# A router kernel's last row: one load in place of two, and three tiles of another split

## The chip, the cores and the metric

The kernel runs on one core of a Trainium2 chip. The metric is the time of one execution on the device in microseconds (us), the median of three runs. A core has TensorE (PE in the profile, its weight loads PEld), VectorE (DVE), ScalarE (ACT), GpSimd (POOL) and SyncE (SP), each with its own queue of instructions, and DMA engines that move data between HBM and the on-chip memory SBUF. Matmuls write into PSUM, from which VectorE and ScalarE read.

## The reference

The kernel computes a softmax over 8 scores per token. There are 16 x 512 = 8192 tokens of 1024 values.

```python
def reference(x: np.ndarray, router_weights: np.ndarray) -> np.ndarray:
    logits = np.matmul(x, router_weights)
    exp_logits = np.exp(logits - np.max(logits, axis=-1, keepdims=True))
    return (exp_logits / np.sum(exp_logits, axis=-1, keepdims=True)).astype(np.float32)
```

x has shape 16 x 512 x 1024 in fp32, router_weights 1024 x 8 in fp32.

## The kernel before

The 8192 tokens are laid out as 128 partitions of J = 64 rows each: partition p holds tokens 64p to 64p + 63. "Block j" is row j of every partition, 128 tokens of 1024 values. A block has KO = 8 column tiles of 128 x 128.

**Loads.** The first four blocks come in fp32 over SP's queue, and ScalarE casts them to bf16. All others are issued by GpSimd, whose DMAs cast to bf16 on the way: twelve loads of four blocks, three of two, five of one (`LOADS`, line 38), and for the last block two loads of 6 and 2 column tiles (`LAST_LOADS`, line 39, issued at line 86). All loads have buffers of their own. From the ninth on, an issue waits for the landing of the load eight before it[...].

**Per block.** `turn` transposes the 8 column tiles on TensorE into a PSUM tile `pt` (line 162, pool `psum_t`, four buffers). `evict` copies it to SBUF as `xT` (line 173). Up to block 53 (`NEAR`) VectorE copies all 1024 columns; after that VectorE takes 640 and ScalarE 384. `project` (line 114) multiplies the eight 128 x 128 pieces with the weights, 8 columns each, accumulating in a logits tile `lg` (pool `psum_l`, three buffers). It lags one or two blocks behind (`pend`). `fill` adds matmuls on constant data in blocks 24 to 59.

**Softmax.** Blocks are grouped for it (`GROUPS`, line 40): six groups of 8, one of 6, one of 8 and the last two blocks alone. The five steps of a group (`peak`, `power`, `total`, `recip`, `scale`) go into the list `later`, from which `step` takes one per block. The last two blocks have a softmax of their own (lines 210 to 223): the peak of each on VectorE (line 214), the exponent on ScalarE (line 215), then sum, reciprocal and scaling on VectorE.

**Order.** The schedule is written out by hand (`manual_schedule`): each engine executes its instructions in the order of the program text. For the last two blocks J-2 and J-1 that order is: transposes and copies of J-2, transposes of J-1 (three `pt` tiles: 4 tiles for VectorE and 2 for ScalarE from the first load, 2 for VectorE from the second), projections of J-2, copies of J-1, projections of J-1.

**Stores.** SP waits for the first of the last two loads by a DMA of two values (`mark`, line 194), then stores blocks 0 to 53 (line 195). The other ten blocks are stored at the very end (line 224).

Of the kernel before, what the change touches and what calls it, by code (L numbers as in the profile page):

```python
# [10 lines left out]
def kernel(  # L11
# [6 lines left out]
    nc = tc.nc  # L18
    P = 128
# [4 lines left out]
    KO = D // P  # L24
    J = M // P


    x_rows = x.rearrange("b s d -> (b s) d").rearrange("(p j) d -> p j d", p=P)
# [3 lines left out]
    bf16 = mybir.dt.bfloat16  # L32
# [2 lines left out]
    ALU = mybir.AluOpType  # L35


    LOADS = [4] * 13 + [2, 2, 2] + [1] * 5
    LAST_LOADS = [6, 2]
    GROUPS = [8] * 6 + [6, 8, 1, 1]  # L40
    assert sum(LOADS) == J - 1 and sum(LAST_LOADS) == KO and sum(GROUPS) == J
    DONE = sum(GROUPS[:7])
    NEAR = 54

# [1 line left out]
    xpool = ctx.enter_context(tc.tile_pool(name="x", bufs=1))  # L46
    xtp = ctx.enter_context(tc.tile_pool(name="xT", bufs=5))
    sm = ctx.enter_context(tc.tile_pool(name="sm", bufs=2))
    psum_t = ctx.enter_context(tc.tile_pool(name="psum_t", bufs=4, space=bass.MemoryType.PSUM))
    psum_f = ctx.enter_context(tc.tile_pool(name="psum_f", bufs=1, space=bass.MemoryType.PSUM))  # L50
    psum_l = ctx.enter_context(tc.tile_pool(name="psum_l", bufs=3, space=bass.MemoryType.PSUM))

    x_of = []
    with tc.manual_schedule():
# [3 lines left out]
        w_bf = const.tile([P, KO, N], bf16)  # L58
# [3 lines left out]

        x_f32 = const.tile([P, LOADS[0], D], fp32)
        for k in range(0, LOADS[0], 2):
            nc.sync.dma_start(out=x_f32[:, k:k + 2, :], in_=x_rows[:, k:k + 2, :])
        nc.scalar.dma_start(
            out=w8[:], in_=router_weights.rearrange("(ko ki) n -> ko ki n", ko=KO)
        )
        j0 = 0
        for i, r in enumerate(LOADS):  # L70
            xb = xpool.tile([P, r, D], bf16, name=f"x_{i}", tag=f"x_{i}")
# [7 lines left out]
            if i == 2:  # L79
                make_identity(nc, ident)  # L80
                nc.gpsimd.memset(filler[:], 0.5)  # L81
        x_last = []
        k0 = 0
        for i, n in enumerate(LAST_LOADS):
            xb = xpool.tile([P, n * P], bf16, name=f"xe_{i}", tag=f"xe_{i}")
            nc.gpsimd.dma_start(out=xb[:], in_=x_rows[:, J - 1, k0 * P:(k0 + n) * P])  # L86
            x_last.append((xb, k0, n))
            k0 += n
        nc.vector.tensor_copy(out=identity[:], in_=ident[:])  # L89
        w_ps = psum_l.tile([P, 8, N], fp32, name="lg")  # L90
        for n in range(N):
# [5 lines left out]
        logits = {}  # L97
# [9 lines left out]
        def project(j, parts):  # L107

            g, k = group_of[j]
            if g not in logits:  # L110
                logits[g] = psum_l.tile([P, 8, N], fp32, name="lg")
            for xT, k0, n in parts:
                for i in range(n):
                    nc.tensor.matmul(  # L114
                        logits[g][:, k, :],
                        lhsT=xT[:, i, :],
                        rhs=w_bf[:, k0 + i, :],
                        start=(k0 + i == 0),
                        stop=(k0 + i == KO - 1),
                    )  # L120
            if k == GROUPS[g] - 1 and j < J - 2:
                softmax(g)

        def softmax(g):
            n, a = GROUPS[g], first[g]
            lg = logits.pop(g)[:, 0:n, :]
            mx = sm.tile([P, n, 1], fp32, name="mx")
            ex = sm.tile([P, n, N], fp32, name="ex")
            ev = sm.tile([P, n, N], fp32, name="ev")
            ssum = sm.tile([P, n, 1], fp32, name="ssum")  # L130
            inv = sm.tile([P, n, 1], fp32, name="inv")

            def peak():
                nc.vector.reduce_max(mx[:, :, 0], lg, axis=X)  # L134

            def power():
                nc.vector.tensor_tensor(  # L137
                    out=ex[:], in0=lg, in1=mx[:].broadcast_to([P, n, N]), op=ALU.subtract
                )
                nc.scalar.activation(ev[:], ex[:], func=Exp)  # L140

            def total():
                nc.vector.reduce_sum(ssum[:, :, 0], ev[:], axis=X)  # L143

            def recip():
                nc.vector.reciprocal(inv[:], ssum[:])  # L146

            def scale():
                nc.vector.tensor_tensor(  # L149
                    out=outv[:, a:a + n, :], in0=ev[:], in1=inv[:].broadcast_to([P, n, N]), op=ALU.mult  # L150
                )

            later.extend([peak, power, total, recip, scale])

        def turn(xb, split, k0=0):

            pts, i = [], 0
            for copy, n in zip((nc.vector.tensor_copy, nc.scalar.copy), split):
                if n:
                    pt = psum_t.tile([P, KO, P], bf16, name="pt")  # L160
                    for c in range(n):
                        nc.tensor.transpose(  # L162
                            pt[:, c, :], xb[:, (i + c) * P:(i + c + 1) * P], identity[:]
                        )
                    pts.append((copy, pt, k0 + i, n))
                    i += n
            return pts

        def evict(pts):
            parts = []  # L170
            for copy, pt, k0, n in pts:
                xT = xtp.tile([P, n, P], bf16, name=f"xT{n}")
                copy(out=xT[:], in_=pt[:, 0:n, :])  # L173
                parts.append((xT, k0, n))
            return parts

        def step(n=1):
            for _ in range(n):
                if later:
                    later.pop(0)()  # L180

        for j in range(J - 2):
            xb, k = x_of[j]
            parts = evict(turn(xb[:, k, :], (KO, 0) if j < NEAR else (5, 3)))
            step()
            pend.append((j, parts))
            while len(pend) > (2 if j < NEAR else 1):
                project(*pend.pop(0))
            if 24 <= j < J - 4:
                fill(2 if j < 48 else 1)  # L190


        mark = const.tile([1, 2], bf16)
        nc.sync.dma_start(out=mark[:], in_=x_last[0][0][0:1, 0:2])
        nc.sync.dma_start(out=out_rows[:, 0:DONE, :], in_=outv[:, 0:DONE, :])


        while pend:
            project(*pend.pop(0))
        step(2)  # L200
        xb, k = x_of[J - 2]
        before = evict(turn(xb[:, k, :], (5, 3)))
        step(1)
        (xa, ka, na), (xb, kb, nb) = x_last
        turned = turn(xa, (4, 2), ka) + turn(xb, (2, 0), kb)
        project(J - 2, before)
        last = evict(turned)
        step(1)
        project(J - 1, last)
        low = sm.tile([P, 2], fp32, name="low")  # L210
        ev = sm.tile([P, 2, N], fp32, name="ev_last")
        for k in range(2):
# [9 lines left out]
            out=outv[:, J - 2:J, :], in0=ev[:], in1=ssum[:].broadcast_to([P, 2, N]), op=ALU.mult  # L222
# [32 lines left out]
```

## Time and profile before

| | |
|---|---|
| median of three runs | 88.85 us (88.81 to 88.88) |
| span of the profiled execution | 87.0 us (time of that run 88.78 us) |
| PE, PEld busy | 73%, 62% |
| DVE, ACT, POOL busy | 55%, 14%, 15% |
| read from HBM | 33.59 MB, 389 GB/s over the span |
| GpSimd's load queue | 15.73 MB written, 88.3% of 16 DMA engines' time |

The span is the time from the first to the last event of the profiled execution on the core; the time of a run contains a little more. The chain of waits follows the work that ended last back to the start, so its shares say what the span is made of. A timeline row gives start, duration, engine, line and operation with the tile written and the tile read, and in brackets the idle time ahead of it and what ended it. A row with "x8" is eight instructions in one piece, and its duration runs from the first one's start to the last one's end.

### The profile page before, as it was taken

How to read it: one execution, taken by the hardware profiler on the slowest of the kernel's cores; microseconds unless marked ns; L12 is line 12 of the kernel's file. 1: busy time of each engine (PE TensorE's matmuls, PEld its weight loads, DVE VectorE, ACT ScalarE, POOL GpSimd, SP SyncE). 2: the span in 40 equal slices, each digit the busy share in tenths (PEclk: the TensorE clock that was granted, in tenths of full speed). 3: DMA queues.
4: the chain of work that ended last, by engine and by line, in shares of the span. 5: the costliest groups of instructions: out<-in, count | busy, mean ns of one | idle time of the engine just before them, and what ended most of it. 6: DMA issues, size and time to landing. Idle time of an engine off the chain costs nothing.

```text
span 87.0 us, 2427 instructions
## 1 busy us (share of the span) xinstructions
PE 63.8 (73%) x1092; PEld 53.6 (62%) x1092; DVE 48.1 (55%) x112; ACT 12.4 (14%) x25; POOL 12.9 (15%) x29
## 2 busy tenths in 40 slices
PE   0408004999396926949999998989898999997730
PEld 0407004999296926947777775757575888795620
DVE  0303300699576663723677677746676589563760
ACT  3235009000100010000010001000100003454540
POOL 5990002020010202020010202020010222000000
PEclk9999999999956999555999999999999999999997
DMA  3899999999999999999999999999999999999520
GB/s 60 328 358 286 260 249 222 222 211 230 196 222 211 222 215 211 226 207 215 218 215 226 200 226 215 207 226 207 226 207 198 220 213 210 202 210 211 88 102 19
DMA packets 3773, 18.26 MB, mean 210 GB/s; under 512 B 556, under 2 KB 940, under 8 KB 1972
## 3 DMA queue, kind: packets, MB, share of 16 engines
q0 software_dynamic: 3168, 15.73, 88.3%
q1 hardware_dynamic: 580, 2.36, 7.3%
q8 instruction: 8, 0.13, 0.5%
q10 hardware_dynamic: 16, 0.03, 0.2%
q14 instruction: 1, 0.01, 0.0%
HBM read 33.59 MB, written 0.26 MB: 389 GB/s over the span
## 4 chain that ended last, share of the span: by engine, by line
DMA 89%; POOL 3%; issue 2%; DVE 1%; PE 1%; ACT 0%; POOLq 0%
DMA x<-in_x_dram 75%; DMA xe<-in_x_dram 14%; POOL x L76 2%; POOL filler L81 1%; DVE xT L173 0%; PE lg L114 0%; PE pt L162 0%; POOL ident masks.py:199 0%; ACT ev_last L215 0%; POOL ident masks.py:197 0%; DVE ssum_last L219 0%; DVE low L214 0%; DVE ssum_last L220 0%; DVE outv L221 0%; POOLq L239 0%
## 5 line engine op out<-in xcount | busy, mean ns | idle before, releaser
L173 DVE COPY xT<-pt 128x1024 bf16<-128x1024 bf16 (+2 forms) x65 | 42.0, 652 | 31.8 <-PE pt L162 31.6
L162 PE MATMUL pt<-identity,x 128*128 128x128 bf16 x504 | 43.4, 236 | 16.0 <-ACT x L74 8.1
L162 PEld LDWEIGHTS <-x 128*128 128x128 bf16 x504 | 34.6, 105 | 25.8 <-DMA x<-in_x_dram 10.9
L114 PE MATMUL lg<-w_bf,xT 128*128 128x8 bf16 x512 | 22.7, 168 | 0.3 <-DVE xT L173 0.2
L114 PEld LDWEIGHTS <-xT 128*128 128x128 bf16 x512 | 20.7, 99 | 0.5 <-DVE xT L173 0.5
L104 PE MATMUL spare<-filler 128*128 128x512 bf16 x60 | 19.2, 384 | 0.0
L76 POOL DMA_DIRECT2D x<-in_x_dram x20 | 10.7, 543 | 56.2 <-DMA x<-in_x_dram 55.4
L140 ACT ACTIVATE ev<-ex 128x64 f32<-128x64 f32 (+1 forms) x8 | 2.0, 255 | 56.2 <-DVE ex L137 56.2
L173 ACT COPY xT<-pt 128x384 bf16<-128x384 bf16 (+1 forms) x10 | 4.7, 467 | 5.1 <-PE pt L162 4.9
L74 ACT CAST x<-x_f 128x1024 bf16<-128x1024 f32 x4 | 4.0, 1042 | 8.5 <-DMA x_f<-in_x_dram 8.5
L104 PEld LDWEIGHTS <-filler 128*128 128x128 bf16 x60 | 4.1, 96 | 0.0
L92 PE MATMUL lg<-ident,w 8*128 8x8 f32 x8 | 1.0, 254 | 3.1 <-POOL ident masks.py:199 3.1
L92 PEld LDWEIGHTS lg<-ident,w 8*128 8x128 f32 x8 | 1.0, 198 | 3.1 <-POOL ident masks.py:199 3.1
L89 DVE CAST identity<-ident 128x128 bf16<-128x128 f32 x1 | 0.5, 512 | 3.0 <-POOL ident masks.py:199 3.0
L134 DVE TENSOR_REDUCE mx<-lg 128x8 f32<-128x64 f32 (+1 forms) x8 | 1.7, 213 | 0.5 <-PE lg L114 0.5
L137 DVE TENSOR_TENSOR ex<-lg,mx 128x64 f32<-128x64 f32 (+1 forms) x8 | 1.7, 213 | 0.0
L149 DVE TENSOR_TENSOR outv<-ev,inv 128x64 f32<-128x64 f32 (+1 forms) x8 | 1.7, 212 | 0.0
L143 DVE TENSOR_REDUCE ssum<-ev 128x8 f32<-128x64 f32 (+1 forms) x8 | 1.7, 208 | 0.0
L86 POOL DMA_DIRECT2D xe<-in_x_dram x2 | 1.1, 527 | 3.9 <-DMA x<-in_x_dram 3.9
L146 DVE RECIPROCAL inv<-ssum 128x8 f32<-128x8 f32 (+1 forms) x8 | 1.5, 191 | 0.0
L74 ACT ACT_TABLE_LOAD x1 | 1.3, 1283 | 1.3 <-PEq L239 1.3
L162 PE MATMUL pt<-identity,xe 128*128 128x128 bf16 x8 | 0.6, 222 | 0.2 <-DMA xe<-in_x_dram 0.2
(14 smaller groups left out, 3.4 us busy)
## 6 DMA issues: line engine op xcount, KB each, us to landing
x<-in_x_dram POOLq DMA_DIRECT2D x12, 1024.0 KB, 35.4
x_f<-in_x_dram SPq DMA_DIRECT2D x2, 1024.0 KB, 8.4
x<-in_x_dram POOLq DMA_DIRECT2D x3, 512.0 KB, 33.9
x<-in_x_dram POOLq DMA_DIRECT2D x5, 256.0 KB, 20.6
out_dram<-outv SPq DMA_DIRECT2D x1, 216.0 KB, 1.9
xe<-in_x_dram POOLq DMA_DIRECT2D x1, 192.0 KB, 11.8
xe<-in_x_dram POOLq DMA_DIRECT2D x1, 64.0 KB, 9.7
out_dram<-outv SPq DMA_DIRECT2D x1, 40.0 KB, 1.5
```

Of the source, the lines that this page charges most:

```text
L74: nc.scalar.copy(xb[:, k, :], x_f32[:, k, :])
L76: nc.gpsimd.dma_start(out=xb[:], in_=x_rows[:, j0:j0 + r, :])
L92: nc.tensor.transpose(w_ps[:, n, :], w8[:, :, n], ident[0:KO, 0:KO])
L104: nc.tensor.matmul(spare[:], lhsT=filler[:, 0:P], rhs=filler[:], start=True, stop=True)
L114: nc.tensor.matmul(logits[g][:, k, :], lhsT=xT[:, i, :], rhs=w_bf[:, k0 + i, :], start=(k0 + i == 0), stop=(k0 + i == KO - 1),)
L134: nc.vector.reduce_max(mx[:, :, 0], lg, axis=X)
L137: nc.vector.tensor_tensor(out=ex[:], in0=lg, in1=mx[:].broadcast_to([P, n, N]), op=ALU.subtract)
L140: nc.scalar.activation(ev[:], ex[:], func=Exp)
L143: nc.vector.reduce_sum(ssum[:, :, 0], ev[:], axis=X)
L149: nc.vector.tensor_tensor(out=outv[:, a:a + n, :], in0=ev[:], in1=inv[:].broadcast_to([P, n, N]), op=ALU.mult)
L162: nc.tensor.transpose(pt[:, c, :], xb[:, (i + c) * P:(i + c + 1) * P], identity[:])
L173: copy(out=xT[:], in_=pt[:, 0:n, :])
```

## The change

The last block comes in one load like the five before it (`LOADS` ends in six ones, `LAST_LOADS` goes). In `turn` the list of engines becomes VectorE, ScalarE, VectorE, and the last block is split 3, 3, 2: VectorE copies 384 columns, ScalarE 384, VectorE 256. `project` takes the parts in the order in which they are given, with the start flag on the first and the stop flag on the last matmul, whichever column tile that is; for the last block both VectorE parts go ahead of ScalarE's. The pool `psum_t` has five buffers instead of four, `psum_l` two instead of three. `mark` reads from the one load.

```diff
-    LOADS = [4] * 13 + [2, 2, 2] + [1] * 5
-    LAST_LOADS = [6, 2]
+    LOADS = [4] * 13 + [2, 2, 2] + [1] * 6
...
-    psum_t = ctx.enter_context(tc.tile_pool(name="psum_t", bufs=4, space=bass.MemoryType.PSUM))
+    psum_t = ctx.enter_context(tc.tile_pool(name="psum_t", bufs=5, space=bass.MemoryType.PSUM))
...
-    psum_l = ctx.enter_context(tc.tile_pool(name="psum_l", bufs=3, space=bass.MemoryType.PSUM))
+    psum_l = ctx.enter_context(tc.tile_pool(name="psum_l", bufs=2, space=bass.MemoryType.PSUM))
...
-        x_last = []
-        k0 = 0
-        for i, n in enumerate(LAST_LOADS):
-            xb = xpool.tile([P, n * P], bf16, name=f"xe_{i}", tag=f"xe_{i}")
-            nc.gpsimd.dma_start(out=xb[:], in_=x_rows[:, J - 1, k0 * P:(k0 + n) * P])
-            x_last.append((xb, k0, n))
-            k0 += n
...
-            for xT, k0, n in parts:
-                for i in range(n):
-                    nc.tensor.matmul(
-                        logits[g][:, k, :],
-                        lhsT=xT[:, i, :],
-                        rhs=w_bf[:, k0 + i, :],
-                        start=(k0 + i == 0),
-                        stop=(k0 + i == KO - 1),
-                    )
+            todo = [(xT[:, i, :], k0 + i) for xT, k0, n in parts for i in range(n)]
+            for i, (xT, ko) in enumerate(todo):
+                nc.tensor.matmul(
+                    logits[g][:, k, :],
+                    lhsT=xT,
+                    rhs=w_bf[:, ko, :],
+                    start=(i == 0),
+                    stop=(i == KO - 1),
+                )
...
-            for copy, n in zip((nc.vector.tensor_copy, nc.scalar.copy), split):
+            for copy, n in zip((nc.vector.tensor_copy, nc.scalar.copy, nc.vector.tensor_copy), split):
...
-        nc.sync.dma_start(out=mark[:], in_=x_last[0][0][0:1, 0:2])
+        nc.sync.dma_start(out=mark[:], in_=x_of[J - 1][0][0:1, 0, 0:2])
...
-        (xa, ka, na), (xb, kb, nb) = x_last
-        turned = turn(xa, (4, 2), ka) + turn(xb, (2, 0), kb)
+        xb, k = x_of[J - 1]
+        turned = turn(xb[:, k, :], (3, 3, 2))
         project(J - 2, before)
-        last = evict(turned)
+        va, sc, vb = evict(turned)
         step(1)
-        project(J - 1, last)
+        project(J - 1, [va, vb, sc])
```

More of the change, by code (lines that the diff above doesn't have):

```diff
@@ L35 @@
     ALU = mybir.AluOpType
-    LOADS = [4] * 13 + [2, 2, 2] + [1] * 5
-    LAST_LOADS = [6, 2]
+    LOADS = [4] * 13 + [2, 2, 2] + [1] * 6
     GROUPS = [8] * 6 + [6, 8, 1, 1]
-    assert sum(LOADS) == J - 1 and sum(LAST_LOADS) == KO and sum(GROUPS) == J
+    assert sum(LOADS) == J and sum(GROUPS) == J
     DONE = sum(GROUPS[:7])
@@ L153, in softmax, with turn @@
             later.extend([peak, power, total, recip, scale])
-        def turn(xb, split, k0=0):
+        def turn(xb, split):
             pts, i = [], 0
-            for copy, n in zip((nc.vector.tensor_copy, nc.scalar.copy), split):
+            for copy, n in zip((nc.vector.tensor_copy, nc.scalar.copy, nc.vector.tensor_copy), split):
                 if n:
@@ L164, in turn @@
                         )
-                    pts.append((copy, pt, k0 + i, n))
+                    pts.append((copy, pt, i, n))
                     i += n
```

## The prediction

> **What bounds the kernel now.** I read the chain of waits first, then its last stretch in order of time, then the timeline of each engine in that stretch, then the table of stretches.
>
> ```profile
> span 87.0 us, 2427 instructions
> ...
> DMA 89%; POOL 3%; issue 2%; DVE 1%; PE 1%; ACT 0%; POOLq 0%
> ```
>
> 89% of the span is loads: from 4.48 us on, the chain is nothing but transfers of x. A change that ends after the stream can only be worth something in what follows the last landing. That stretch in order of time (start, duration, what):
>
> ```profile
> 70.27 11.84 DMA xe<-in_x_dram
> 82.11 0.05 issue
> 82.16 0.41 PE pt L162 x4
> 82.57 0.02 issue
> 82.59 0.43 DVE xT L173
> 83.03 0.05 issue
> 83.07 0.42 PE lg L114 x8
> 83.49 0.02 issue
> 83.51 0.18 DVE low L214
> ```
>
> The first part of the last row (6 of 8 column tiles) lands at 70.27 + 11.84 = 82.11. Everything after is serial: 4 transposes, VectorE's copy of 512 columns, 8 projections, then the softmax of two blocks and the store, 83.51 to 87.0 = 3.49 us, with no idle time to absorb a shift. What stands beside that chain, first the weight loads of TensorE:
>
> ```profile
> 78.70 0.45 PEld L162 LDWEIGHTS <-x 128*128 128x128 bf16 x8 [0.40 <-DMA x<-in_x_dram]
> ...
> 79.97 0.45 PEld L162 LDWEIGHTS <-x 128*128 128x128 bf16 x8 [0.56 <-DMA x<-in_x_dram]
> ...
> 82.15 0.47 PEld L162 LDWEIGHTS <-xe 128*128 128x128 bf16 x8 [0.41 <-DMA xe<-in_x_dram]
> ```
>
> All 8 transposes of the last row run in one piece, so the second load (2 tiles) never made TensorE wait, although it lands later: its issue stands at 72.72, and the shortest of the two flights was 9.7, which makes 82.42.
>
> ```profile
> 72.72 0.53 POOL L86 DMA_DIRECT2D xe<-in_x_dram  x1 [1.93 <-DMA x<-in_x_dram]
> ...
> DMA to landing us min/median/max: 9.7/10.8/11.8
> ```
>
> Then the copies out of PSUM on VectorE and on ScalarE; ScalarE's row holds that of block J-2 and that of J-1 behind it:
>
> ```profile
> 82.59 0.62 DVE L173 COPY xT<-pt 128x512 bf16<-128x512 bf16 x2
> ...
> 82.17 0.91 ACT L173 COPY xT<-pt 128x384 bf16<-128x384 bf16 x2
> ```
>
> [...] So with one load no transpose of the last row can start on the first six tiles. The trace agrees with the kernel before: the transposes start 0.05 us after the first load's landing. [...] so ScalarE's last copy stands behind its copy of block J-2, and the order of projections matters. The trace agrees: it shows no instruction overtaking another.
>
> **The change part by part.** Times are those of the profiled execution (span 87.0, reported as 88.78 us; the three timed runs: 88.81 to 88.88). A shift of the tail moves both by the same microseconds.
>
> *One load for two.* Removed: one issue on POOL (0.53 us, at 72.72) and its wait of 1.93; nothing is queued behind it on POOL, and the data of the last rows fly about 10 us after issue, so this is worth 0. The first issue stays where it is, behind the same loads. Landing: at the end of the stream rows of 1024 columns come 79.97 - 78.70 = 1.27 us apart by the weight loads that waited for them. The first load (6 tiles, 3/4 of a row) was in at 82.11; the missing quarter takes 0.25 x 1.27 = 0.32, so the whole is in at 82.43. The other way: the same bytes were in at 82.42 with two loads. I take 82.42, a start 0.31 later. Bounds: if the second load's 0.31 were overhead and not bytes, the landing would be 82.11 (shift 0); if one load takes what the longest spacing gives, 82.50 (shift 0.39).
>
> *Three tiles of 3, 3, 2.* Transposes start at 82.42 + 0.05 = 82.47. In the chain 4 of them took 0.41, from the first start to the end; one more costs 0.06 (starts of 8 weight loads span 0.47, the last one itself some 0.10, so about 0.37/7 to 0.06). Three end at 82.82, six at 83.00, eight at 83.12. VectorE's copy of 384: the groups by shape show 281 ns for 256 columns and 423 for 512, so 352 between them: 82.84 to 83.19. ScalarE's copy of 384: the four late ones have a mean of 475 ns: 83.02 to 83.50. It replaces one of 372 ns for 256 columns. VectorE's 256: 83.17 to 83.45 (two VectorE copies together 0.63 against 0.70). ScalarE therefore ends last, 0.05 after VectorE. Before, VectorE was last at 82.59 + 0.62 = 83.21, ScalarE at 83.08.
>
> *Projections.* TensorE has the 8 of block J-2 first (weight loads 82.94 to 83.25), which is hidden before the last block's. Then VectorE's three and two, then ScalarE's three from 83.50 + 0.05 = 83.55. Eight took 0.42 in the chain, each further one 0.03 (weight loads of 8 span 0.31 including one of 0.10), so three take 0.42 - 5 x 0.03 = 0.27: end 83.82 against 83.49. In the order 0 to 7, the two VectorE tiles would come last, another 0.06; the order of arrival saves this and no more.
>
> *Accumulating order and PSUM pools.* Other start and stop flags on the same number of matmuls: 0. Five buffers for transposes in place of four: before, the third tile of the last block had to wait for VectorE's copy of block J-2 (ended 82.37), and its transposes came at about 82.53, so no wait is removed; 0, and in the stream the loads hide it. Two logits buffers in place of three: block J-1's logits now take the buffer of the group of blocks 54 to 61, whose last reader, VectorE's subtraction, ends at 81.75 + 0.23 = 81.98; the first projection comes after 83.2. In the loop a group's buffer is read out two steps after its last projection and wanted eight blocks later. Both 0, at most a short wait in the first blocks, hidden behind loads.
>
> *SP queue.* The mark (0.70 us) waits for the whole row, so it and the 216 KB store behind it move from 82.13 to about 82.44 and from 82.88 to 83.19. That store lands 1.9 us after issue, 85.1; the last store is issued at 84.62 + 0.32 = 84.94 and lands 1.5 us later, 86.4. SP is free at 83.55, so nobody waits: 0.
>
> Sum: the landing +0.31; the rest nets +0.02 (fewer transposes ahead and a shorter VectorE copy, against ScalarE's longer copy that now ends last), which is inside the rounding of these rows, so I take +0.31. Reciprocal of the group before (0.19) would start at 83.37 and block J-2's peak follows at about 83.48 to 83.65, ahead of the last peak at 83.83: no new wait. Span 87.0 to 87.3; time 88.85 + 0.31 = 89.16. Own range 89.02 (landing 82.33, other errors -0.08) to 89.30 (landing 82.50, copies +0.06).
>
> **The rivals.** *No change, the row lands as early as its first part did.* If the small load was all overhead, transposes start at 82.16, ScalarE's copy runs from 82.71 to 83.19, projections end at 83.24 + 0.27 = 83.51, 0.02 later than before: 88.87. For it: the second load's reads are short (1 KB against 3 KB of a row). Against it: 0.94 us for three quarters of a row and 0.31 for a quarter are just their shares of 1.27. This also shows that landing early wins nothing: in the limit ScalarE's copy of J-2 ends at 82.17 + 0.46 = 82.63, then 0.48 + 0.05 + 0.27 gives 83.43, only 0.06 better.
>
> *Faster: the stream itself ends sooner.* Place: the DMA queues behind POOL; the short packets of the second load are in them together with those of rows J-3 and J-2 and could slow these too. Price: to be faster by 0.18 the projections must end at 83.31. Going back by 0.27, 0.05, 0.48 and 0.53 from there, row J-1 must be in before 81.93, 0.49 earlier than I reckon, and ScalarE must be through with J-2's copy by 82.51, 0.12 earlier. That copy stands behind the exponent of the group that ends with row J-3, so J-3 must land sooner as well. At twice this gain the time would be 88.5. For it: small packets are the only thing on the queues that changes. Against it: the whole second load holds 0.31 us of the stream, less than the 0.49 wanted, and the DMA share is full (207 to 214 GB/s from 70 to 80 us).
>
> *Slower by more: the tail is pushed further.* The later 216 KB store runs into the last store on SP's queue, or ScalarE's copy also delays block J-2's exponent. Price: the last store's landing moves by up to 0.2 more: 89.36. Against it: between 85.1 and 85.9 the queue has room. That the change doesn't do what it says is excluded by the order of instructions: one load, copies of 384, 256 and 384, projections in the order stated.
>
> **How the numbers follow.** A measurement of this kernel can tell 0.2%, 0.18 us, from no change (the three runs span 0.07). Tail later by 0.3: 0.70, and slower by more: 0.08, both slower by over 0.2%: 0.78. Row lands with its first part: 0.12, within 0.2%. Stream sooner: 0.10, faster. Range 88.85 to 89.36: it holds the forecast, the rival of no change from 88.85 on and most of the slower one, and leaves out the faster one.
>
> **What would show it.** Right: transposes of the last row start near 82.47 after a wait of 0.7 or so for the load; ScalarE's 384 copy ends last, near 83.5; last projections end near 83.8; everything after keeps its durations. Wrong: transposes starting before 82.3, a ScalarE copy that is not the last releaser of the projections, any wait of TensorE for a logits buffer, or a stream that reaches block J-2 at another time than 81.2.

## The result and the profile after

The changed kernel takes 89.16 us (median of six runs, 88.96 to 89.22), the kernel before beside it 88.84 us: a ratio of 1.0033, 95% interval 1.0020 to 1.0046. It is 0.32 us slower. The forecast was 89.16 us.

The profiled execution (89.21 us) has a span of 87.4 us against 87.0. Here is its page's first line, and its chain of waits by engine:

```profile
span 87.4 us, 2415 instructions
...
DMA 86%; issue 4%; POOL 3%; PE 2%; DVE 1%; ACT 0%; POOLq 0%
```

The span is still made of loads. (Loads had 89% before. The chain of this profile counts 1.96 us ahead of the last load's issue as "issue".) The end of the chain in order of time (start, duration, what):

```profile
70.34 12.15 DMA x<-in_x_dram
82.49 0.05 issue
82.54 0.62 PE pt L154 x8
83.16 0.76 PE lg L106 x16
83.92 0.02 issue
83.94 0.18 DVE low L206
```

The last load is issued at 70.34, as the first of the two was at 70.27, but its flight, the time from issue to landing, is 12.15 us instead of 11.84: 0.31 longer, to 82.49. Projections end at 83.92 instead of 83.49. These 0.43 are 0.31 of flight, 0.07 of a later issue, and 0.05 after the landing, from which it is 1.43 us to the end of projections in place of 1.38. From there on every piece of the chain has its old duration to 0.01. The rest of the span is 3.48 us, before it was 3.51, with spans rounded to 0.1.

This chain strings TensorE's transposes and projections together, since TensorE shows no gap. What released the last three projections is not visible in it. The timelines of VectorE and ScalarE show that:

```profile
82.92 0.57 DVE L165 COPY xT<-pt 128x384 bf16<-128x384 bf16 x2
```

```profile
82.41 0.48 ACT L165 COPY xT<-pt 128x384 bf16<-128x384 bf16 x1
83.14 0.48 ACT L165 COPY xT<-pt 128x384 bf16<-128x384 bf16 x1 [0.25 <-PE pt L154]
```

VectorE is through with both its tiles at 82.92 + 0.57 = 83.49, ScalarE with its one at 83.14 + 0.48 = 83.62. The last projections follow ScalarE: 83.62 to 83.92 is 0.30, made of a start 0.05 later and 0.25 for three matmuls.

The weight loads show how the last two blocks met their loads:

```profile
81.69 0.45 PEld L154 LDWEIGHTS <-x 128*128 128x128 bf16 x8 [0.34 <-DMA x<-in_x_dram]
82.53 0.45 PEld L154 LDWEIGHTS <-x 128*128 128x128 bf16 x8 [0.39 <-DMA x<-in_x_dram]
```

In the kernel before, the loads for block J-2 started at 81.28 and waited for nothing:

```profile
81.28 0.46 PEld L162 LDWEIGHTS <-x 128*128 128x128 bf16 x8
```

So in this execution block J-2 came about 0.4 later than in the profile before. The prediction named just this, a stream that reaches block J-2 at another time than 81.2, as a sign of being wrong, and by its letter that sign came. It didn't move the last row: the first experiment below has J-2 in time (its loads start at 81.26) and the same flight of 12.15 us for the last load.

### The profile page after: what moved, and what is told of

Read it like the earlier page. It is cut to its first block, busy times and chain, and to the rows that moved or that the text cites. A ratio compares the mean times of both kernels' runs of the same rounds, so it can differ in the third digit from the quotient of the medians.

```text
span 87.4 us, 2415 instructions
## 1 busy us (share of the span) xinstructions
PE 63.3 (72%) x1080; PEld 53.6 (61%) x1092; DVE 47.9 (55%) x112; ACT 12.6 (14%) x25; POOL 12.4 (14%) x28
## 4 chain that ended last, share of the span: by engine, by line
DMA 86%; issue 4%; POOL 3%; PE 2%; DVE 1%; ACT 0%; POOLq 0%
DMA x<-in_x_dram 86%; POOL x L75 2%; PE lg L106 1%; PE pt L154 1%; POOL filler L80 1%; POOL ident masks.py:199 0%; ACT ev_last L207 0%; POOL ident masks.py:197 0%; DVE ssum_last L211 0%; DVE ssum_last L212 0%; DVE low L206 0%; DVE outv L213 0%; POOLq L242 0%; POOLq L231 0%
## 5 line engine op out<-in xcount | busy, mean ns | idle before, releaser
L154 PE MATMUL pt<-identity,x 128*128 128x128 bf16 x512 | 43.9, 236 | 16.6 <-DMA x<-in_x_dram 8.5
L154 PEld LDWEIGHTS <-x 128*128 128x128 bf16 x512 | 35.1, 105 | 26.5 <-DMA x<-in_x_dram 11.9
L75 POOL DMA_DIRECT2D x<-in_x_dram x21 | 11.3, 543 | 58.2 <-DMA x<-in_x_dram 57.4
L96 PE MATMUL spare<-filler 128*128 128x512 bf16 x48 | 16.1, 391 | 0.6
L165 ACT COPY xT<-pt 128x384 bf16<-128x384 bf16 x10 | 4.8, 479 | 5.4 <-PE pt L154 5.2
L207 ACT ACTIVATE ev_last<-lg,low 128x8 f32<-128x8 f32 x2 | 0.5, 268 | 0.3 <-DVE low L206 0.2
```

What stands on the lines that cost most here:

```text
L75: nc.gpsimd.dma_start(out=xb[:], in_=x_rows[:, j0:j0 + r, :])
L96: nc.tensor.matmul(spare[:], lhsT=filler[:, 0:P], rhs=filler[:], start=True, stop=True)
L154: nc.tensor.transpose(pt[:, c, :], xb[:, (i + c) * P:(i + c + 1) * P], identity[:])
```

## The experiments

All kernels were timed beside the kernel before on the same chip. Times over the kernel before are differences of medians.

**One load, old division.** From the changed kernel:

```diff
-        turned = turn(xb[:, k, :], (3, 3, 2))
+        turned = turn(xb[:, k, :], (4, 2, 2))
...
-        project(J - 1, [va, vb, sc])
+        project(J - 1, [va, sc, vb])
```

> The changed kernel with the old division of the last block (VectorE 512 columns, ScalarE 256, VectorE 256) and its projections in the order of the text; the row still comes in one load. Theory (the whole row must land before its first transpose, the rest nets about nothing): time near 89.15 us, 0.25 to 0.35 over the kernel before, transposes from about 82.5. Rival (ScalarE's longer copy of 384 columns is the cost): back to within 0.05 of the kernel before, 88.85 to 88.90.

Measured: 89.09 against 88.78 us, ratio 1.0031 (1.0017 to 1.0045): 0.31 us slower. Taking back the division leaves the whole loss in place, so ScalarE's longer copy is not its cause.

**Two loads, new division, order and pools.** From the kernel before, with the changed `project`:

```diff
-    psum_t = ctx.enter_context(tc.tile_pool(name="psum_t", bufs=4, space=bass.MemoryType.PSUM))
+    psum_t = ctx.enter_context(tc.tile_pool(name="psum_t", bufs=5, space=bass.MemoryType.PSUM))
...
-    psum_l = ctx.enter_context(tc.tile_pool(name="psum_l", bufs=3, space=bass.MemoryType.PSUM))
+    psum_l = ctx.enter_context(tc.tile_pool(name="psum_l", bufs=2, space=bass.MemoryType.PSUM))
...
-        turned = turn(xa, (4, 2), ka) + turn(xb, (2, 0), kb)
+        turned = turn(xa, (3, 3), ka) + turn(xb, (2, 0), kb)
...
-        project(J - 1, last)
+        project(J - 1, [va, vb, sc])
```

> The kernel before with its two loads (6 and 2 column tiles), but the new division 384, 384, 256, the projections in the order of arrival and the new PSUM pools. Theory: within 0.06 of the kernel before (projections end at 83.50, before 83.49). Rival (the longer copy on ScalarE is the cost): near 89.15.

Measured: 88.80 against 88.78, ratio 0.9999 (0.9983 to 1.0014). Everything in the change except the load is together not to be told from 0, within 0.15 us either way. The chain of this run's trace:

```profile
70.16 11.84 DMA xe<-in_x_dram
82.00 0.05 issue
82.04 0.64 PE pt L162 x8
82.68 0.74 PE lg L114 x16
```

The load of six tiles flies 11.84 us again, and from its landing to the end of projections (82.68 + 0.74 = 83.42) it is 1.42, against 83.49 - 82.11 = 1.38 before.

**The two loads in the opposite order.** From the kernel before:

```diff
-        k0 = 0
-        for i, n in enumerate(LAST_LOADS):
+        for i, (k0, n) in enumerate([(LAST_LOADS[0], LAST_LOADS[1]), (0, LAST_LOADS[0])]):
...
-            x_last.append((xb, k0, n))
-            k0 += n
+            x_last.insert(0, (xb, k0, n))
```

> The kernel before with its two loads in the opposite order: the load of 2 column tiles is issued first, that of 6, which the first transposes need, last. Number and sizes of the loads, division and pools are those of before. Theory (what counts is when the last bytes that the first transpose needs are in): transposes from about 82.5, time 0.28 to 0.36 over the kernel before, near 89.17. Rival (one large load as such, its longer descriptors or its single issue, is the cost): within 0.05 of the kernel before.

Measured: 89.25 against 88.78, ratio 1.0041 (1.0026 to 1.0055): 0.46 slower. Here the number of loads, their sizes and the tail are those of before. Only the load that the first transposes need is now the last one:

```profile
72.63 9.74 DMA xe<-in_x_dram
82.38 0.05 issue
82.42 0.41 PE pt L160 x4
82.83 0.02 issue
82.86 0.44 DVE xT L171
```

It lands at 82.38, and copy and projections follow as before. One large load as such is thus not needed for the loss: it is enough that the first transpose waits for the last bytes of the row. The profiled execution (89.04) stood 0.26 over that of before, the median 0.46. The interval, 0.23 to 0.49 us, holds the expected 0.28 to 0.36 too; the gap is taken up below.

**The PSUM pools alone.** From the kernel before:

```diff
-    psum_t = ctx.enter_context(tc.tile_pool(name="psum_t", bufs=4, space=bass.MemoryType.PSUM))
+    psum_t = ctx.enter_context(tc.tile_pool(name="psum_t", bufs=5, space=bass.MemoryType.PSUM))
...
-    psum_l = ctx.enter_context(tc.tile_pool(name="psum_l", bufs=3, space=bass.MemoryType.PSUM))
+    psum_l = ctx.enter_context(tc.tile_pool(name="psum_l", bufs=2, space=bass.MemoryType.PSUM))
```

> The kernel before with five buffers for transposes and two for logits, nothing else. Theory: 0, within 0.05 of the kernel before. Rival (a wait for a logits buffer or for a transposed tile comes or goes): off by 0.1 or more, with a wait of TensorE for VectorE in the trace of blocks 54 to 63.

Measured: 88.80 against 88.78, ratio 0.9992 (0.9978 to 1.0006): nothing that can be told. In the trace TensorE waits for VectorE's copy where it did before, 0.33 us at 81.01 in both.

**The projections in the order of the columns.** From the changed kernel:

```diff
-        project(J - 1, [va, vb, sc])
+        project(J - 1, [va, sc, vb])
```

> The changed kernel with the last projections in the order of the columns (VectorE's three, ScalarE's three, VectorE's two) in place of the order of arrival. Theory (ScalarE's tile is in last; the two matmuls left behind it come one by one 0.03 us apart): 0.06 over the changed kernel, near 89.2, not clear of it. Rival (the order is what the change lives by): 0.2 or more over the changed kernel.

Measured: 89.24 against 88.78, ratio 1.0048 (1.0033 to 1.0062). This interval overlaps the changed kernel's own (1.0020 to 1.0046), so the times don't tell the two apart. The trace does give a price. Its chain:

```profile
82.60 0.52 PE pt L154 x6
83.12 0.02 issue
83.14 0.02 ACTq L165
83.16 0.04 issue
83.20 0.49 ACT xT L165
83.69 0.05 issue
83.73 0.29 PE lg L106 x5
```

Five matmuls stand behind ScalarE's tile and take 0.29 us, against 0.25 for three in the changed kernel: the order of arrival saves some 0.04 us. (The granted clock was halved during part of those three, from 83.77 us on. In the repeat of the changed kernel, at the full clock, it is 0.29 from the end of ScalarE's copy to the end of projections, here 0.34.)

**More distance: the last two rows in one load.** From the changed kernel:

```diff
-    LOADS = [4] * 13 + [2, 2, 2] + [1] * 6
+    LOADS = [4] * 13 + [2, 2, 2] + [1] * 4 + [2]
```

> The changed kernel with its last two rows in one load, so that block J-2 too can start only when the last bytes are in. Theory (the tail starts at the landing of what its first transpose needs): both rows land at about 82.42, 16 transposes, the copies of both blocks and all projections follow, end of projections near 84.5 against 83.5 before: time 0.8 to 1.1 over the kernel before, near 89.8. Rival (fewer, larger loads end the stream sooner): landing before 82.2, time below 89.5.

Measured: 89.94 against 88.78, ratio 1.0113 (1.0079 to 1.0146): 1.16 slower, a little over the upper end expected. The chain:

```profile
67.77 14.55 DMA x<-in_x_dram
82.32 0.05 issue
82.37 1.07 PE pt L154 x16
83.44 0.85 PE lg L106 x16
84.29 0.02 issue
```

The last bytes are in at 82.32, within 0.1 of the 82.42 with two loads, so larger loads did not end the stream visibly sooner. The transposes of both blocks now start only then, and projections end at 84.29, 0.80 later than before. That is the whole of the loss of this execution (89.58 against 88.78). The six executions lie between 89.53 and 90.22; what adds the other 0.36 in the median, this trace doesn't show.

**Three loads.** From the kernel before:

```diff
-    LAST_LOADS = [6, 2]
+    LAST_LOADS = [4, 2, 2]
...
-        (xa, ka, na), (xb, kb, nb) = x_last
-        turned = turn(xa, (4, 2), ka) + turn(xb, (2, 0), kb)
+        (xa, ka, na), (xb, kb, nb), (xc, kc, nc_) = x_last
+        turned = turn(xa, (4, 0), ka) + turn(xb, (0, 2), kb) + turn(xc, (2, 0), kc)
```

> The kernel before with its last row in three loads of 4, 2 and 2 column tiles, VectorE copying the first four, ScalarE the next two, VectorE the last two, as before. Theory: the four tiles are in at about 81.8, the last two at 82.45 to 82.5; what then ends last is VectorE's copy of the last two: projections end near 83.42 against 83.49, time 0 to 0.1 below the kernel before, hardly to be told from it. Rival (each further small load costs the stream a fixed time of 0.1 or more): at or over the kernel before.

Measured: 88.74 against 88.78, ratio 0.9997 (0.9983 to 1.0012). Nothing that can be told. A third load costs the stream nothing visible, and an earlier first part brings nothing visible. In the profiled execution (88.89, over the median) projections ended at 83.61 and not at the expected 83.42. Its chain shows what took the place of the load:

```profile
82.19 0.50 DVE xT L173
82.69 0.04 issue
82.73 0.27 PE pt L162 x2
```

The last two transposes wait for VectorE's copy of block J-2, whose PSUM buffer they take (four buffers here); the third load was already in at 75.15 + 7.3 = 82.45. But this is an execution in which block J-2 landed late: its loads start at 81.69, as in the changed kernel's profile. In the kernel before, where J-2 was in time, the same copy ended at 82.37, ahead of such a third load. So the trace doesn't say which of the two waits is the usual one.

**A halved clock?** In the profile of the first experiment the granted clock fell just after the load had landed at 82.39. The table of stretches (stretch, length, then busy us of PE, PEld, DVE, ACT, POOL with counts, granted clock, DMA share, GB/s):

```profile
82.00:82.50 0.50, 0.07 (x1) 0.07 (x2) 0.48 (x2) 0.50 (x2) 0.00 (x0) 1.00 0.00 0
82.50:83.00 0.50, 0.50 (x7) 0.50 (x8) 0.03 (x1) 0.10 (x1) 0.00 (x0) 0.60 0.00 0
83.00:83.50 0.50, 0.50 (x13) 0.50 (x11) 0.50 (x2) 0.32 (x1) 0.00 (x0) 0.50 0.00 0
```

In that execution the eight transposes took 0.93 us in place of 0.62, and the span was 87.5. Since TensorE now waits longer for the last row (0.72 us ahead of its weight loads there, 0.41 in the kernel before), it was a fair question whether this is part of the loss. That a longer wait lowers the clock was only my guess. The first kernel that asked it was the changed one with one constant matmul more:

```diff
+        fill(1)
         turned = turn(xb[:, k, :], (3, 3, 2))
```

> The changed kernel with one constant matmul more on TensorE (0.38 us at the full clock) between the transposes of block J-2 and those of the last row, where TensorE waits for the load. It ends before the load lands. Theory (the wait for the whole row is the cost; the clock is a side effect of it): time within 0.1 of the changed kernel, still 0.2 to 0.3 over the kernel before. Rival (TensorE idles longer, so its clock is halved for the last transposes and projections, as one profile with one load showed, and that is a good part of the cost): within 0.1 of the kernel before.

Measured: 89.12 against 88.78, ratio 1.0037 (1.0021 to 1.0054). That is 0.34 over it: no gain that can be told. Then four kernels on one chip: the changed kernel unaltered, the opposite order once more, and both with two constant matmuls more. They were to tell two theories apart that explain why the opposite order's median stood 0.46 over and its profile only 0.26. Theory A: in part of the executions the clock is halved in the tail, since TensorE waits longer, and that adds to the loss. Theory B: the difference was chance. The two matmuls more are this edit:

```diff
-            if 24 <= j < J - 4:
+            if 24 <= j < J - 3:
...
+        fill(1)
```

> The changed kernel once more, unaltered, beside the next three on one chip. Both theories: 0.3 to 0.4 over the kernel before.

> The two loads in the opposite order once more. Its profile stood 0.26 over that of the kernel before, its median 0.46. Theory A (in part of its executions TensorE's clock is halved in the tail, since it waits longer for the load): the median lies 0.35 to 0.5 over the kernel before and the times spread over 0.3 us. Theory B (the difference was chance): 0.25 to 0.35 over it.

> The two loads in the opposite order with two constant matmuls more, one after block J-4 and one while TensorE waits for the last row; both end before the data they precede have landed. Theory A (halved clock): 0.25 to 0.32 over the kernel before, less than without them by 0.1 or more, and less spread. Theory B: no difference to the kernel without them.

> The changed kernel with the same two constant matmuls more. Theory A (halved clock adds to the cost of the later landing in part of the executions): 0.05 to 0.1 below the changed kernel, 0.28 or so over the kernel before. Theory B: as the changed kernel. On neither does it come down to the kernel before.

Measured, against 88.95 us of the kernel before on this chip:

| kernel | median, us | over before | ratio, 95% interval |
|---|---|---|---|
| changed kernel again | 89.34 | 0.39 | 1.0040 (1.0027 to 1.0054) |
| opposite order again | 89.34 | 0.39 | 1.0042 (1.0028 to 1.0056) |
| opposite order, two matmuls more | 89.30 | 0.35 | 1.0038 (1.0024 to 1.0052) |
| changed kernel, two matmuls more | 89.31 | 0.36 | 1.0036 (1.0023 to 1.0049) |

The medians don't show theory A: the matmuls take off 0.04 and 0.03 us, within the intervals. The profiles of the two repeats speak against it as a cause of the loss. At 89.33 and 89.42 us they are as slow as the medians of their kernels or slower, yet the clock stood at 1.00 until TensorE was through. This is the changed kernel again, whose projections end at 84.04:

```profile
83.00:83.50 0.50, 0.50 (x16) 0.42 (x13) 0.46 (x2) 0.23 (x1) 0.00 (x0) 1.00 0.00 0
83.50:84.00 0.50, 0.50 (x8) 0.35 (x8) 0.25 (x3) 0.46 (x2) 0.00 (x0) 1.00 0.00 0
```

From landing to the end of projections it is 1.42 us here and 1.38 in the opposite order, within 0.01 as in their first profiles. What was later is the issue of the last load: 70.48 against 70.34, and 72.98 against 72.63.

The single executions do hold a hint for theory A. Each has a granted clock, averaged over its whole span. Split at 0.935 (a limit chosen with the result known), the 22 executions of the opposite order in its first experiment have medians of 89.04 above and 89.32 below it, those of one load with the old division 89.06 and 89.31, those of the kernel before 88.76 and 88.86. At the higher clock the loss against the kernel before is thus still 0.28 and 0.30 us, which the clock cannot explain; that a lower one adds some tenths in part of the executions is possible. The average doesn't say when the clock fell, and the ten executions of the changed kernel's repeat show no such difference (89.34 on both sides), so this stays open.

The more important result is another: the kernel with two loads in the opposite order and the changed kernel are equally slow, 0.39 us each.

## Why the prediction was right, step by step

**What bounds.** Right. The stream ends in the same place with one, two or three loads for the last row, within what the issue times differ: at 82.49, 82.42 and 82.45 in the profiles of the changed kernel, of the kernel before and of three loads. The loss is that the 1.4 us from the landing to the end of projections start later; they are hardly longer.

**One load for two.** Right in mechanism and size. I took the whole row to be in 0.31 after its first six tiles, as a quarter of 1.27 us. Measured were 12.15 us of flight against 11.84. All six profiles with one load for the last row have 12.14 or 12.15, the three with the load of six tiles first 11.84 to 11.87. In the profile the landing stands at 82.49 rather than 82.42, since the load was issued 0.07 later. That no transpose of the row starts before its load is in, the prediction took as given; in the six profiles with one load the transposes start 0.04 or 0.05 after the landing, in the changed kernel at 82.54 after 82.49. This is what costs here: by the difference of the two flights, the last 0.31 of the 12.15 us are for two tiles, and the first six have to wait for them. Fewer, larger transfers brought nothing here: three loads cost no more than two (88.74 us against 88.78), and one load ended the stream no sooner.

**Three tiles of 3, 3, 2.** The view of these copies gives their durations (minimum, median and maximum in ns):

```profile
L165 DVE COPY xT<-pt x2: 292/325/358, 82.9 to 83.2; 128x384 bf16<-128x384 bf16 x1, 128x256 bf16<-128x256 bf16 x1
L165 ACTq EVENT_SEMAPHORE  x1: 17/17/17, 83.1 to 83.1; - x1
L165 ACT COPY xT<-pt x1: 479/479/479, 83.1 to 83.1; 128x384 bf16<-128x384 bf16 x1
```

VectorE's copy of 384 columns took 358 ns (estimated 352), its copy of 256 now 292 (281), ScalarE's of 384 took 479 (475). One term was missing. From the end of the sixth transpose to the start of ScalarE's copy I had 0.02, the pause that the chain shows between a TensorE and a VectorE instruction. In the changed kernel a separate instruction of ScalarE's queue, the EVENT_SEMAPHORE above, stands ahead of that copy; in the kernel before, none stands ahead of its last one. The chain of the order experiment shows it between the two: 83.12 to 83.20 is 0.08. What it waits for, the trace doesn't show. So ScalarE's tile was 0.06 later than I had it. I had the end of projections 0.33 after that of before and it was 0.43 in the profile: 0.07 from the issue and 0.06 from this gap, less 0.02 for the last three matmuls (0.25 in place of 0.27) and 0.01 of rounding.

**Projections, pools, SP queue.** As costed. The order of arrival is worth 0.04 or 0.05 (0.06 reckoned), the pools nothing that can be told. The mark was issued at 82.51 and the last store at 85.05, 0.43 after 84.62, which is the shift of the projections and no more.

**The rivals.** "No change" fell with the flight of 12.15 us. "The stream ends sooner" would have needed the last row before 81.93; it was in at 82.49, and with two rows in one load at 82.32. "Slower by more" did not come: the tail after the projections kept its length, 3.48 us in place of 3.51.

**Sum.** Forecast +0.31, measured +0.32 by the timed runs and +0.39 when repeated on another chip. That the first agrees to 0.01 is partly luck. The flight gives 0.31 and the longer wait and copy of ScalarE 0.05 more, 0.36 in all; the forecast left the second part out as rounding. And the profiled execution of the same kernel was 0.43 above that of before.

## What to carry to other kernels

In this kernel, where loads make up 89% of the span before, what counted was when the bytes were in that the first instruction after it needs, and how much work was left then; the number of loads mattered here much less than which piece came last (three loads 0.04 us under the kernel before; one load and the opposite order each 0.39 over it in the repeats). In such a case, cut the last transfer so that the long serial part starts on the first piece, and let the second piece arrive while engines are busy with the first: 0.31 us of flight were hidden that way, and one load puts them back on the path. Cutting further brought nothing visible here; in the one profile of it, the copy ahead and its PSUM buffer had become the wait, to 82.69, with the third load in at 82.45.

## What the runs showed of the hardware that was not expected

In two profiles the granted TensorE clock fell to half while TensorE was still at work on the last rows: at 82.60 us with one load and the old division, and at 83.77 in the changed kernel. In the kernel before it stood at 1.00 from 41.36 to 85.73, and TensorE was through at 83.49. Within one profile the changes of the clock lie whole steps apart. From 30 us on they stand at 32.57, 39.40, 42.81 and 83.77 in the changed kernel, that is 2, 1 and 12 steps of 3.41 us apart; in the kernel before at 34.53, 41.36 and 85.73, 2 and 13 steps. Equal kernels differ in where it falls: in the repeated run of the changed kernel the clock stayed at 1.00 to 84.50 at least, past the end of projections at 84.04. The length of TensorE's waits doesn't foretell the drops: in the 3.41 us before them the longest wait of its weight loads was 0.72 us with one load and the old division and 0.39 in the changed kernel, and with the opposite order the clock stayed at 1.00 to 84.00 after a wait of 0.77. TensorE's matmuls were busy for 79% of the 3.41 us before the drop in the changed kernel, as the profile counts them, and in the kernel before the clock held after a step (78.91 to 82.32) with 72%. So neither these waits nor the busy share alone explains the drops; what does stays open.

The row of block J-2 was late in three of the profiles. Its flight was 13.8 us in the changed kernel and 13.9 in the one with three loads, against 13.4 in the kernel before. TensorE's loads for it then start at 81.69 in both, and with one constant matmul more at 81.53 after a wait of 0.37 for this row; in the kernel before they start at 81.28 and wait for nothing. The last row wasn't late in these: its last bytes were in at 82.49, 82.45 and 82.30. The cause was not tried.
